# Paired activation parts in the first feed-forward product, and the second norm's sums at a later place, in a two-layer decoder trunk

## The chip, the cores and the metric

The kernel runs on one core of one Trainium2 chip. The metric is device time in microseconds for one execution of the whole program, as the median of several runs. Besides the runs there is one profiled execution, from which all the rows below come.

## The reference, cut to what matters

The input x is 256 tokens by 1024, float32. Two layers each do a normed, gated mix of three token mixers with a residual, and then the feed-forward part, which is where the change lies:

```python
def rms_norm(x, g):
    y = x * lax.rsqrt(jnp.mean(x * x, axis=-1, keepdims=True) + NORM_EPS)
    return y * g

x = x + (g_a * o_a + g_b * o_b + g_c * o_c) @ w_out
h = rms_norm(x, g_ffn)
x = x + jnp.square(jax.nn.relu(h @ w_ff1)) @ w_ff2      # 1024 -> 4096 -> 1024
```

The norm's factor of a row is positive, so it passes through Relu and comes out of the square as its square: the kernel multiplies by g_ffn only, runs both products without the row factor, and multiplies the end result by 1/(mean of squares + eps).

## The kernel before, in words

**Split products.** For float32 accuracy every weight and every activation is held as two parts, hi (the value rounded to the PE's fp32r form) and lo (the rest). A product is three matmuls that add up in one PSUM bank: hi x hi, hi x lo, lo x hi. `gemm_b` (lines 163 to 169) does it with the weights stationary and 256 activation columns moving: line 167 is weight hi with activation hi, 168 weight hi with activation lo, 169 weight lo with activation hi. `gemm_a` (171 to 177) does it with the activations stationary and 512 weight columns moving (lines 175 to 177).

**Weights.** `piece` (143 to 159) fetches 512 KB into a raw buffer (tag raw, five buffers, issued by SP at line 138), ACT writes the hi part (line 157) and DVE the lo part (line 158). Ring 0 has four hi and four lo buffers and holds the first product's weights; ring 1 takes its buffers from the five of tag big.

**PSUM.** `psum` (line 95) hands out whole banks: two of tag mm, two at, two pt, one po, one ch, eight in all. A bank goes to its next user only when everything that reads it is done.

**The feed-forward stage.** After the output projection, `transposed` (203 to 213) transposes x block by block (128 tokens) and writes its hi part (ACT, line 211) and lo part (DVE, line 212), times g_ffn, to h2 and l2, two tiles of 8 x 256 columns. The inner dimension of 4096 is worked in NG = 16 groups of 256, gi = 0 to 15 in the code; the texts below use gi. `ff1(gi)` (893 to 908) runs the first product of a group: two halves u of 128 inner channels, each over 8 chunks k of the model dimension, 2 x 8 x 3 = 48 matmuls into the two halves of one mm bank. In group 0 all u do k 0 to 3 first and then k 4 to 7. Then the result is evacuated: line 903 (ACT) r = Relu, 905 (ACT) rh = Square of r, 906 (DVE) r = max(ps, 0) x r, which reads the bank once more and writes over the r that 905 reads, 907 (DVE) rl = r - rh.

The second product, `acc_pass` (868 to 873), adds a group's part into the four banks po4, two blocks b of tokens by two halves n of the output: 24 matmuls of 512 columns per group. The loop of line 918 issues ff1(gi + 1) ahead of the second product of gi; the second products of the last three groups are kept for the end, so that the first products of groups 14 and 15 run back to back. At the end line 936 (DVE) multiplies by the row factor r2 and adds the residual.

**The second norm's sums.** Lines 912 to 916: for each block `sumsq_row` (232 to 242) does two Squares of 128x512 with an accumulated sum on ACT (line 239), an add and a scale on DVE (240, 241); line 915 takes the reciprocal. They stand between ff1(0) and ff1(1) in the program.

**Order.** Each engine runs its own queue in order. The order in a queue is made ahead of time by a planner that takes, at each point, the oldest instruction whose inputs and buffers it believes to be ready; so an instruction that is younger in the program can stand before an older one that had to wait.

Of the kernel before, what the change touches and what calls it, by code (L numbers as in the profile page):

```python
# [8 lines left out]
F32 = mybir.dt.float32  # L9
R32 = mybir.dt.float32r  # L10
BF16 = mybir.dt.bfloat16
I32 = mybir.dt.int32
AF = mybir.ActivationFunctionType
ALU = mybir.AluOpType
AX = mybir.AxisListType

P = 128
D = 1024
T = 256
NB = T // P  # L20
# [65 lines left out]
def trunk_kernel(ctx: ExitStack, tc: tile.TileContext, A, out, depth=DEPTH):  # L86
    nc = tc.nc
# [3 lines left out]
    ap_ = ctx.enter_context(tc.tile_pool(name="ap", bufs=1))  # L91
# [3 lines left out]
    def psum(tag, name):  # L95
        return pp.tile([P, 512], F32, tag=tag, name=name, bufs={"mm": 2, "at": 2, "pt": 2, "po": 1, "ch": 1}[tag])

    def stat(n, name, dt=F32):
        return sp.tile([P, n], dt, tag="st%d" % n, name=name, bufs=2 if n > 64 else 6)
# [7 lines left out]
    mm = nc.tensor.matmul  # L107
# [35 lines left out]
    def piece(src, k, ring=0, half=0):  # L143

        n = src.shape[-1]
        r = raw(src, n)
        if ring == 0:
            hi = wp.tile([P, 1024], R32, tag="hi", name="hi", bufs=WB)[:, :n]
            if not ringgap:
                ringgap.append(wp.tile([P, 64], F32, tag="gap6", name="gap6", bufs=1))  # L150
            lo = wp.tile([P, 1024], R32, tag="lo", name="lo", bufs=WB)[:, :n]
        else:
            if half == 0:
                ring2[0] = (ap_.tile([P, 2048], R32, tag="big", name="hi2", bufs=BIG),
                            ap_.tile([P, 2048], R32, tag="big", name="lo2", bufs=BIG))
            hi, lo = (t[:, half * 1024:half * 1024 + n] for t in ring2[0])
        act(hi, r, AF.Copy)  # L157
        tt(out=lo, in0=r, in1=hi.bitcast(F32), op=ALU.subtract)  # L158
        return tuple(t.rearrange("p (k n) -> p k n", k=k) for t in (hi, lo))
# [3 lines left out]
    def gemm_b(ps, wh, wl, ah, al, ks, first=True, last=True):  # L163

        n = len(ks)
        for i, (kw, ka) in enumerate(ks):
            mm(ps, lhsT=wh(kw), rhs=ah(ka), start=(first and i == 0), stop=False)  # L167
            mm(ps, lhsT=wh(kw), rhs=al(ka), start=False, stop=False)  # L168
            mm(ps, lhsT=wl(kw), rhs=ah(ka), start=False, stop=(last and i == n - 1))  # L169

    def gemm_a(ps, ah, al, wh, wl, ks, first=True, last=True):

        n = len(ks)
        for i, (kw, ka) in enumerate(ks):
            mm(ps, lhsT=ah(ka), rhs=wh(kw), start=(first and i == 0), stop=False)  # L175
            mm(ps, lhsT=ah(ka), rhs=wl(kw), start=False, stop=False)  # L176
            mm(ps, lhsT=al(ka), rhs=wh(kw), start=False, stop=(last and i == n - 1))  # L177

    def split(hi, lo, src):
        splits[0] = act(hi, src, AF.Copy)  # L180
        splits[1] = tt(out=lo, in0=src, in1=hi.bitcast(F32), op=ALU.subtract)
# [18 lines left out]
                stt(out=y, in0=t, scalar=1.5, in1=y, op0=ALU.add, op1=ALU.mult)  # L200
        return y

    def transposed(src, b, g, hh, hl, name, c0):

        pt = psum("pt", name)
        for c in range(c0, c0 + 4):
            nc.tensor.transpose(pt[:, (c - c0) * P:(c - c0 + 1) * P], src[:, c * P:(c + 1) * P], ident)
        for c in range(c0, c0 + 4):
            pc = pt[:, (c - c0) * P:(c - c0 + 1) * P]
            hc = hh[:, c, b * P:(b + 1) * P]  # L210
            act(hc, pc, AF.Copy, scale=g[:, c:c + 1])
            stt(out=hl[:, c, b * P:(b + 1) * P], in0=pc, scalar=g[:, c:c + 1], in1=hc.bitcast(F32),
                op0=ALU.mult, op1=ALU.subtract)

    scaled = [None]
# [45 lines left out]
    def layer(l):  # L261
# [4 lines left out]
        def K(n, i=None):  # L266
            o, w = COL[n]
            return cols[:, o:o + w] if i is None else cols[:, o + i:o + i + 1]
# [5 lines left out]
        def s2(shape, name, dt=F32):  # L274
            return sp.tile(shape, dt, tag="s2", bufs=S2, name=name)
# [4 lines left out]
        def pa(name, dt=F32):  # L280
            return sp.tile([P, 512], dt, tag="pa", bufs=PA, name=name)
# [2 lines left out]
        hA = lambda t, b: (lambda k: t[:, k, b * P:(b + 1) * P])  # L284
        col = lambda ap: ap.rearrange("p (n o) -> p n o", o=1)


        if l == 0:

            ap_.tile([P, 48], F32, tag="gap0", name="gap0")  # L290
        hh = ap_.tile([P, 8, T], R32, tag="hh", name="hh", bufs=2)
        hl = ap_.tile([P, 8, T], R32, tag="hl", name="hl", bufs=2)
        grow = raw(bass.AP(tensor=A["gmix"].tensor, offset=A["gmix"].offset + l * D, ap=[[0, P], [1, D]]), D)
        vs = stat(2, "n1v")
        for b in range(NB):
# [246 lines left out]
        oh = ol = None  # L542
# [291 lines left out]
        def gated(m, c2):  # L834

            nonlocal mh, ml
            g = gslice(m, c2)
            ps = w_o(("wo_mla", "wconv", "wo_nsa")[m], *((oh, ol, 0), (yh, yl, 0), (oh, ol, 4))[m], c2)
            if m == 1:
                ob = s2([P, 512], "ob")  # L840
                for u in range(2):
                    act(ob[:, u * T:(u + 1) * T], ps[:, u * T:(u + 1) * T], AF.Identity, bias=K("bco", 2 * c2 + u))
                ps = ob
            stt(out=g, in0=g, scalar=1.0, in1=ps, op0=ALU.add, op1=ALU.mult)
            if done[c2]:
                tt(out=g, in0=gslice(done[c2][-1], c2), in1=g, op=ALU.add)
            done[c2].append(m)
            if len(done[c2]) == 3:
                if mh is None:
                    mh = ap_.tile([P, 8, T], R32, tag="hh", name="mh", bufs=2)  # L850
                    ml = ap_.tile([P, 8, T], R32, tag="hl", name="ml", bufs=2)
                c = 2 * c2
                split(mh[:, c:c + 2].rearrange("p c t -> p (c t)"), ml[:, c:c + 2].rearrange("p c t -> p (c t)"), g)

        oh = ap_.tile([P, 8, T], R32, tag="hh", name="oh", bufs=2)
        ol = ap_.tile([P, 8, T], R32, tag="hl", name="ol", bufs=2)
        steps = {"a": a_products, "a0": a_compressed, "a1": a_keys, "a2": a_queries, "qk": nsa_qk, "glu": glu, "lr": low_rank, "lrn": low_rank_norm, "ckv": compress_kv, "csc": compress_scores,
                 "nsa": lambda j: nsa_attention(j, (oh, ol)), "mla": lambda j: mla_attention(j, (oh, ol)),
                 "rk": rotary_keys, "mq": mla_q, "mk": mla_k, "tap": lambda i: taps(TAPS[i], TAPS[i + 1]), "cn": conv_norm,
# [14 lines left out]

        po4 = [[psum("at", "wo0"), psum("at", "wo1")], [psum("po", "wo2"), psum("ch", "wo3")]]
        held = [(k, k) + piece(A["w_out"][l, k], 1, ring=k // 4, half=k % 2) for k in range(8)]
        h2 = ap_.tile([P, 8, T], R32, tag="hh", name="h2", bufs=2)
        l2 = ap_.tile([P, 8, T], R32, tag="hl", name="l2", bufs=2)
        for b in range(NB):
            if b == 0:  # L880
                acc_pass(po4, held, mh, ml, 8, b)
            for n in range(2):
                if b == 1:
                    acc_pass(po4, held, mh, ml, 8, b, (n,))
                xs = x[:, b, n * 512:(n + 1) * 512]
                stt(out=xs, in0=po4[b][n], scalar=0.5, in1=xs, op0=ALU.mult, op1=ALU.add)
                transposed(x[:, b], b, K("gffn"), h2, l2, "n2t", 4 * n)

        po4 = [[psum("at", "f0"), psum("at", "f1")], [psum("po", "f2"), psum("ch", "f3")]]
        NG = 16  # L890
        tail = 3

        def ff1(gi):
            ps = psum("mm", "ff1")
            ws = [piece(A["ff1"][l, 2 * gi + u], 8) for u in range(2)]

            for k0, k1 in ((0, 4), (4, 8)) if gi == 0 else ((0, 8),):
                for u in range(2):
                    wh, wl = ws[u]
                    gemm_b(ps[:, u * T:(u + 1) * T], lambda k: wh[:, k, :], lambda k: wl[:, k, :], hB(h2), hB(l2),  # L900
                           [(k, k) for k in range(k0, k1)], first=(k0 == 0 and (u == 0 or gi > 0)), last=(k1 == 8 and (u == 1 or gi > 0)))
            r = s2([P, 512], "r")
            act(r, ps, AF.Relu)
            rhf, rlf = pa("rh", R32), pa("rl", R32)
            act(rhf, r, AF.Square)  # L905
            stt(out=r, in0=ps, scalar=0.0, in1=r, op0=ALU.max, op1=ALU.mult)
            tt(out=rlf, in0=r, in1=rhf.bitcast(F32), op=ALU.subtract)  # L907
            return tuple(t.rearrange("p (c t) -> p c t", c=2) for t in (rhf, rlf))

        rs = [ff1(0)]  # L910
        r2 = []
        for b in range(NB):
            v = sumsq_row(b, "n2", stat(1, "n2_v"))
            rv = stat(1, "rv")
            nc.vector.reciprocal(rv, v)
            r2.append(rv)
        held = []
        for gi in range(NG):
            if gi + 1 < NG:
                rs.append(ff1(gi + 1))  # L920
            held.append([(2 * gi + u, u) + piece(A["ff2"][l, 2 * gi + u], 1, ring=int(gi < NG - tail + 2), half=u) for u in range(2)])
            if gi < NG - tail:
                for b in range(NB):
                    acc_pass(po4, held[gi], rs[gi][0], rs[gi][1], 2 * NG, b)
# [146 lines left out]
```

## Time and profile before

| what | value |
|---|---|
| time, median of 3 runs | 919.6 us (918.56 to 919.87) |
| the profiled execution's own time | 919.41 us |
| its span, first to last instruction | 917.5 us |
| PE matmul busy | 894.5 us, 97% of the span, 6214 matmuls |
| DVE, ACT busy | 641.9 us (70%), 536.9 us (59%) |
| mean granted TensorE clock | 0.996 of full speed |
| DMA | 151.55 MB, mean 165 GB/s |

Times in the rows count from the span's start. PE is the matmul row of TensorE, PEld its weight loads, DVE the vector engine, ACT the scalar engine, SP the queue that issues the DMAs. L167 is line 167 of the kernel. Matmuls overlap in the pipeline, and their ends are modelled; the start times are measured. An idle time in brackets is followed by what ended it. The feed-forward stages run from 282 to 460 us and from 733 us to the end.

### The profile page before, as it was taken

The numbers are of one execution on the slowest core, as the hardware profiler recorded it, in microseconds if no ns is written. First come the engines' busy times: TensorE is split into PE (matmuls) and PEld (weight loads), VectorE is DVE, ScalarE is ACT, GpSimd is POOL, SyncE is SP. The second block draws the span as 40 slices with busy tenths as digits, with TensorE's granted clock in tenths as the row PEclk, the third lists the DMA queues.
The fourth block names the chain that finished last, engine by engine and source line by source line (L and its number), as shares of the span: only waits on it lengthen the run. The fifth ranks groups of instructions, "written<-read, shape, count | busy, mean of one in ns | idle before, by whom it ended". The sixth has DMA issues, their size and how long they took to land.

```text
span 917.5 us, 16102 instructions
## 1 busy us (share of the span) xinstructions
PE 894.5 (97%) x6214; PEld 794.1 (87%) x6214; DVE 641.9 (70%) x1431; ACT 536.9 (59%) x987; POOL 28.2 (3%) x80
## 2 busy tenths in 40 slices
PE   5999999999999999999999999999999999999998
PEld 4899888689988999999878989877999889999996
DVE  6599988875787665555576999879558785555552
ACT  5456566897467544444354675679865575444430
POOL 4210000000000000000001000000000000000000
PEclk9999999999999999999999999999999999999999
DMA  8654622334656666555355464125436476566621
GB/s 290 217 163 146 221 88 81 115 116 147 186 197 206 217 200 196 191 184 184 103 167 199 162 208 119 61 81 184 160 99 197 151 256 217 185 190 194 190 93 46
DMA packets 43133, 151.55 MB, mean 165 GB/s; under 512 B 4784, under 2 KB 5680, under 8 KB 43056
## 3 DMA queue, kind: packets, MB, share of 16 engines
q1 hardware_dynamic: 43056, 150.52, 50.1%
q8 instruction: 49, 0.80, 0.4%
q14 instruction: 28, 0.23, 0.1%
HBM read 149.45 MB, written 1.05 MB: 164 GB/s over the span
## 4 chain that ended last, share of the span: by engine, by line
PE 86%; DVE 6%; ACT 4%; DMA 3%; issue 1%; SPq 0%; DVEq 0%; ACTq 0%
PE psB L167 7%; PE psB L169 6%; PE psB L168 6%; PE f L177 6%; PE f L175 6%; PE f L176 6%; PE ff L169 6%; PE ff L167 6%; PE ff L168 6%; DVE lo L158 3%; PE wo L167 2%; PE wo L168 2%; PE wo L169 2%; PE nS L589 2%; PE psA L176 2%; ACT hi L157 2%
## 5 line engine op out<-in xcount | busy, mean ns | idle before, releaser
L158 DVE TENSOR_TENSOR lo<-raw,hi 128x1024 fp32r<-128x1024 f32 (+1 forms) x266 | 317.5, 1209 | 168.3 <-ACT hi L157 136.6
L157 ACT ACTIVATE hi<-raw 128x1024 fp32r<-128x1024 f32 (+1 forms) x266 | 273.4, 1048 | 248.1 <-DMA raw<-in_ff_dram 107.3
L167 PE MATMUL psB<-hh,hi 128*128 128x256 f32 x592 | 171.2, 289 | 1.7 <-ACT ug L764 1.4
L169 PE MATMUL psB<-hh,lo 128*128 128x256 f32 x592 | 168.9, 287 | 0.0
L168 PE MATMUL psB<-hl,hi 128*128 128x256 f32 x592 | 168.2, 284 | 0.0
L167 PE MATMUL ff<-h,hi 128*128 128x256 f32 x512 | 143.4, 281 | 0.0
L169 PE MATMUL ff<-h,lo 128*128 128x256 f32 x512 | 143.4, 281 | 0.0
L168 PE MATMUL ff<-l,hi 128*128 128x256 f32 x512 | 143.2, 281 | 0.0
L167 PEld LDWEIGHTS psB<-hh,hi 128*128 128x128 f32 x592 | 112.5, 190 | 8.5 <-issue 4.4
L169 PEld LDWEIGHTS psB<-hh,lo 128*128 128x128 f32 x592 | 112.6, 191 | 3.0 <-issue 2.6
L168 PEld LDWEIGHTS psB<-hl,hi 128*128 128x128 f32 x592 | 112.6, 190 | 0.3
L773 DVE SCALAR_TENSOR_TENSOR ca<-upad,cols,ca 128x256 f32<-128x256 f32 x240 | 103.6, 476 | 0.3
L177 PE MATMUL f<-hi,rl 128*128 128x512 f32 x256 | 100.1, 391 | 1.4 <-DVE n_v L241 1.4
L175 PE MATMUL f<-hi,rh 128*128 128x512 f32 x256 | 100.5, 393 | 0.7 <-ACT rh L905 0.7
L176 PE MATMUL f<-lo,rh 128*128 128x512 f32 x256 | 100.1, 391 | 0.0
L168 PEld LDWEIGHTS ff<-l,hi 128*128 128x128 f32 x512 | 97.8, 191 | 1.0
L167 PEld LDWEIGHTS ff<-h,hi 128*128 128x128 f32 x512 | 96.0, 188 | 1.1
L169 PEld LDWEIGHTS ff<-h,lo 128*128 128x128 f32 x512 | 96.0, 188 | 0.0
L177 PEld LDWEIGHTS f<-hi,rl 128*128 128x128 f32 x256 | 48.1, 188 | 13.0 <-DVE rl L907 2.6
L175 PEld LDWEIGHTS f<-hi,rh 128*128 128x128 f32 x256 | 48.1, 188 | 10.2 <-ACT rh L905 1.1
L176 PEld LDWEIGHTS f<-lo,rh 128*128 128x128 f32 x256 | 48.2, 188 | 9.1
L176 PE MATMUL psA<-lo,hh 128*128 128x512 f32 (+1 forms) x96 | 36.2, 377 | 1.3 <-DVE lo L158 1.3
(279 smaller groups left out, 1421.5 us busy)
## 6 DMA issues: line engine op xcount, KB each, us to landing
raw<-in_ff_dram SPq DMA_DIRECT2D x128, 512.0 KB, 4.1
raw<-in_wB_dram SPq DMA_DIRECT2D x74, 512.0 KB, 3.8
raw<-in_wA_dram SPq DMA_DIRECT2D x16, 512.0 KB, 4.2
raw<-in_w_out_dram SPq DMA_DIRECT2D x16, 512.0 KB, 4.1
raw<-in_wo_nsa_dram SPq DMA_DIRECT2D x8, 512.0 KB, 5.0
raw<-in_wo_mla_dram SPq DMA_DIRECT2D x8, 512.0 KB, 4.4
raw<-in_wconv_dram SPq DMA_DIRECT2D x8, 512.0 KB, 3.8
raw<-in_wA_dram SPq DMA_DIRECT2D x8, 312.0 KB, 5.3
```

Source lines behind the costliest of these rows:

```text
L157: act(hi, r, AF.Copy)
L158: tt(out=lo, in0=r, in1=hi.bitcast(F32), op=ALU.subtract)
L167: mm(ps, lhsT=wh(kw), rhs=ah(ka), start=(first and i == 0), stop=False)
L168: mm(ps, lhsT=wh(kw), rhs=al(ka), start=False, stop=False)
L169: mm(ps, lhsT=wl(kw), rhs=ah(ka), start=False, stop=(last and i == n - 1))
L175: mm(ps, lhsT=ah(ka), rhs=wh(kw), start=(first and i == 0), stop=False)
L176: mm(ps, lhsT=ah(ka), rhs=wl(kw), start=False, stop=False)
L177: mm(ps, lhsT=al(ka), rhs=wh(kw), start=False, stop=(last and i == n - 1))
L589: mm(pS[g].rearrange("p (h z k) -> p h z k", h=nj, z=2)[:, i], lhsT=qTn[gs, 2 * jp + j, b * P:(b + 1) * P], rhs=kTn[gs, :, 0:nk], start=Tr ...
L773: stt(out=ca[:, i], in0=upad[:, i, k:k + T], scalar=K("wdw", 31 * i + k), in1=ca[:, i], op0=ALU.mult, op1=ALU.add)
```

## The change

`ff1` of group 0 stays as it is. In groups 1 to 15 `gemm_p` runs, for each k, one matmul of weight hi with 512 columns, the hi and the lo part of the activations side by side, and one of weight lo with the 256 hi columns, added into the first half of the bank. A half u then fills a whole bank, so a group takes both mm banks. The evacuation adds the two halves of each bank (a copy on ACT and an add on DVE per u), then squares with Relu on DVE and copies the hi part on ACT. For this the hi and lo parts of all activations of that size lie in one tile of [128, 8, 2, 256] instead of two of [128, 8, 256], in as many buffers. The sums of the second norm are issued in the loop, block 0 at gi = 4 and block 1 at gi = 6, behind the weight pieces of that group's second product and ahead of the product; the reciprocal gets a tag of its own.

```diff
+    def gemm_p(ps, wh, wl, a, ks, first=True, last=True):
+
+        n = len(ks)
+        for i, (kw, ka) in enumerate(ks):
+            mm(ps, lhsT=wh(kw), rhs=a[:, ka].rearrange("p s t -> p (s t)"), start=(first and i == 0), stop=False)
+            mm(ps[:, :T], lhsT=wl(kw), rhs=a[:, ka, 0], start=False, stop=(last and i == n - 1))
...
-    def transposed(src, b, g, hh, hl, name, c0):
+    def transposed(src, b, g, h, name, c0):
...
-            hc = hh[:, c, b * P:(b + 1) * P]
+            hc = h[:, c, 0, b * P:(b + 1) * P]
...
+        def pair(name):
+
+            return ap_.tile([P, 8, 2, T], R32, tag="hp", name=name, bufs=2)
...
-        hh = ap_.tile([P, 8, T], R32, tag="hh", name="hh", bufs=2)
-        hl = ap_.tile([P, 8, T], R32, tag="hl", name="hl", bufs=2)
+        hp = pair("hp")
+        hh, hl = hp[:, :, 0], hp[:, :, 1]
...
         def ff1(gi):
-            ps = psum("mm", "ff1")
             ws = [piece(A["ff1"][l, 2 * gi + u], 8) for u in range(2)]
...
+            r = s2([P, 512], "r")
+            rhf, rlf = pa("rh", R32), pa("rl", R32)
+            if gi == 0:
...
+            else:
+                pss = [psum("mm", "ff1") for _ in range(2)]
                 for u in range(2):
                     wh, wl = ws[u]
...
+                    gemm_p(pss[u], lambda k: wh[:, k, :], lambda k: wl[:, k, :], h2, [(k, k) for k in range(8)])
+                for u in range(2):
+                    rt = r[:, u * T:(u + 1) * T]
+                    act(rt, pss[u][:, :T], AF.Copy)
+                    tt(out=rt, in0=pss[u][:, T:], in1=rt, op=ALU.add)
+                stt(out=r, in0=r, scalar=0.0, in1=r, op0=ALU.max, op1=ALU.mult)
+                act(rhf, r, AF.Copy)
             tt(out=rlf, in0=r, in1=rhf.bitcast(F32), op=ALU.subtract)
...
-        for b in range(NB):
-            v = sumsq_row(b, "n2", stat(1, "n2_v"))
-            rv = stat(1, "rv")
-            nc.vector.reciprocal(rv, v)
-            r2.append(rv)
...
+            if gi in (4, 6):
+
+                v = sumsq_row(len(r2), "n2", stat(1, "n2_v"))
+                rv = sp.tile([P, 1], F32, tag="rv", name="rv", bufs=2)
+                nc.vector.reciprocal(rv, v)
+                r2.append(rv)
```

The branch of group 0 holds the old lines, with the old order of k and one bank.

## Rows read from the trace of the kernel before

**Rows 1.** The page, busy time of each engine: us (share of span) xinstructions.
```profile
PE 894.5 (97%) x6214; PEld 794.1 (87%) x6214; DVE 641.9 (70%) x1431; ACT 536.9 (59%) x987; POOL 28.2 (3%) x80
```
**Rows 2.** The page, the chain that ended last, by engine.
```profile
PE 86%; DVE 6%; ACT 4%; DMA 3%; issue 1%; SPq 0%; DVEq 0%; ACTq 0%
```
**Rows 3.** Windows, ten groups: stretch, length, busy us by engine, clock, DMA share, GB/s.
```profile
312.05:423.25 111.20, 111.20 (x721) 101.64 (x720) 62.64 (x64) 52.34 (x60) 0.00 (x0) 1.00 0.61 194
```
**Rows 4.** Timeline, PE, one even group: start, us, engine, line, operation, tiles.
```profile
334.29 0.28 PE L167 MATMUL ff<-h,hi 128*128 128x256 f32 x1
...
339.83 0.28 PE L169 MATMUL ff<-h,lo 128*128 128x256 f32 x1
...
339.94 0.40 PE L175 MATMUL f<-hi,rh 128*128 128x512 f32 x1
...
340.18 0.40 PE L176 MATMUL f<-lo,rh 128*128 128x512 f32 x1
...
341.10 0.39 PE L177 MATMUL f<-hi,rl 128*128 128x512 f32 x1
...
342.46 0.39 PE L177 MATMUL f<-hi,rl 128*128 128x512 f32 x1
```
**Rows 5.** Timeline, PE, group 0 of layer 0.
```profile
284.20 0.28 PE L167 MATMUL ff<-h,hi 128*128 128x256 f32 x1
...
285.56 0.28 PE L167 MATMUL ff<-h,hi 128*128 128x256 f32 x1
```
**Rows 6.** Timeline, ACT, layer 0, around the evacuation of group 0.
```profile
291.63 1.06 ACT L157 ACTIVATE hi<-raw 128x1024 fp32r<-128x1024 f32 x1 [0.29 <-DMA raw<-in_ff_dram]
292.59 0.58 ACT L903 ACTIVATE r<-ff 128x512 f32<-128x512 f32 x1
293.07 0.63 ACT L239 ACTIVATE n_q<-x 128x512 f32<-128x512 f32 x1
...
293.68 0.62 ACT L905 ACTIVATE rh<-r 128x512 fp32r<-128x512 f32 x1
```
**Rows 7.** Timeline, DVE, the last read of group 0's bank.
```profile
294.34 0.69 DVE L906 SCALAR_TENSOR_TENSOR r<-ff,r 128x512 f32<-128x512 f32 x1 [0.39 <-ACT rh L905]
```
**Rows 8.** Timeline, PE, layer 0: last first product of group 1, third second product.
```profile
293.68 0.28 PE L169 MATMUL ff<-h,lo 128*128 128x256 f32 x1
...
295.81 0.50 PE L177 MATMUL f<-hi,rl 128*128 128x512 f32 x1 [0.72 <-DVE n_v L241]
```
**Rows 9.** Timeline, ACT, layer 0, between r and rh of group 1.
```profile
297.47 1.05 ACT L157 ACTIVATE hi<-raw 128x1024 fp32r<-128x1024 f32 x1
298.42 0.62 ACT L905 ACTIVATE rh<-r 128x512 fp32r<-128x512 f32 x1
```
**Rows 10.** Timeline, ACT and PE, the same place in layer 1.
```profile
743.56 0.58 ACT L903 ACTIVATE r<-ff 128x512 f32<-128x512 f32 x1
...
744.77 0.28 PE L169 MATMUL ff<-h,lo 128*128 128x256 f32 x1
...
746.78 0.50 PE L177 MATMUL f<-hi,rl 128*128 128x512 f32 x1 [0.72 <-DVE n_v L241]
```
**Rows 11.** Timeline, ACT and DVE, layer 0, behind the first product of group 14.
```profile
440.11 1.06 ACT L157 ACTIVATE hi<-raw 128x1024 fp32r<-128x1024 f32 x1 [1.77 <-PE ff L168]
441.07 0.58 ACT L903 ACTIVATE r<-ff 128x512 f32<-128x512 f32 x1
...
441.20 1.23 DVE L158 TENSOR_TENSOR lo<-raw,hi 128x1024 fp32r<-128x1024 f32 x1 [1.60 <-ACT hi L157]
```
**Rows 12.** Windows, columns as in rows 3, the stretch at the lower clock.
```profile
119.80:123.20 3.40, 3.40 (x18) 3.40 (x18) 3.30 (x10) 1.71 (x3) 0.12 (x1) 0.50 0.68 171
```
**Rows 13.** Timeline, PE, just before that stretch.
```profile
117.89 1.97 PE L515 MATMUL cS<-kbd,qTn 128*128 128x32 f32 x16
```
**Rows 14.** Windows, a stretch with PE waiting, start of layer 1.
```profile
470.50:473.90 3.40, 1.84 (x8) 0.98 (x7) 1.66 (x3) 1.54 (x2) 0.00 (x0) 1.00 0.85 335
```
**Rows 15.** Timeline, DVE, the last lo part of the activations, layer 0.
```profile
288.11 0.35 DVE L212 SCALAR_TENSOR_TENSOR l<-n2t,cols,h 128x128 fp32r<-128x128 f32 x1 [0.43 <-ACT h L211]
```

More of the change, by code (lines that the diff above doesn't have):

```diff
@@ L209, in transposed @@
             pc = pt[:, (c - c0) * P:(c - c0 + 1) * P]
-            hc = hh[:, c, b * P:(b + 1) * P]
+            hc = h[:, c, 0, b * P:(b + 1) * P]
             act(hc, pc, AF.Copy, scale=g[:, c:c + 1])
-            stt(out=hl[:, c, b * P:(b + 1) * P], in0=pc, scalar=g[:, c:c + 1], in1=hc.bitcast(F32),
+            stt(out=h[:, c, 1, b * P:(b + 1) * P], in0=pc, scalar=g[:, c:c + 1], in1=hc.bitcast(F32),
                 op0=ALU.mult, op1=ALU.subtract)
@@ L849, in gated @@
                 if mh is None:
-                    mh = ap_.tile([P, 8, T], R32, tag="hh", name="mh", bufs=2)
-                    ml = ap_.tile([P, 8, T], R32, tag="hl", name="ml", bufs=2)
+                    mp = pair("mp")
+                    mh, ml = mp[:, :, 0], mp[:, :, 1]
                 c = 2 * c2
-                split(mh[:, c:c + 2].rearrange("p c t -> p (c t)"), ml[:, c:c + 2].rearrange("p c t -> p (c t)"), g)
-        oh = ap_.tile([P, 8, T], R32, tag="hh", name="oh", bufs=2)
-        ol = ap_.tile([P, 8, T], R32, tag="hl", name="ol", bufs=2)
+                split(mh[:, c:c + 2], ml[:, c:c + 2], g.rearrange("p (c t) -> p c t", c=2))
+        op = pair("op")
+        oh, ol = op[:, :, 0], op[:, :, 1]
         steps = {"a": a_products, "a0": a_compressed, "a1": a_keys, "a2": a_queries, "qk": nsa_qk, "glu": glu, "lr": low_rank, "lrn": low_rank_norm, "ckv": compress_kv, "csc": compress_scores,
@@ L876, in layer @@
         held = [(k, k) + piece(A["w_out"][l, k], 1, ring=k // 4, half=k % 2) for k in range(8)]
-        h2 = ap_.tile([P, 8, T], R32, tag="hh", name="h2", bufs=2)
-        l2 = ap_.tile([P, 8, T], R32, tag="hl", name="l2", bufs=2)
+        h2 = pair("h2")
         for b in range(NB):
@@ L886, in layer @@
                 stt(out=xs, in0=po4[b][n], scalar=0.5, in1=xs, op0=ALU.mult, op1=ALU.add)
-                transposed(x[:, b], b, K("gffn"), h2, l2, "n2t", 4 * n)
+                transposed(x[:, b], b, K("gffn"), h2, "n2t", 4 * n)
         po4 = [[psum("at", "f0"), psum("at", "f1")], [psum("po", "f2"), psum("ch", "f3")]]
@@ L893, in ff1 @@
         def ff1(gi):
-            ps = psum("mm", "ff1")
             ws = [piece(A["ff1"][l, 2 * gi + u], 8) for u in range(2)]
-            for k0, k1 in ((0, 4), (4, 8)) if gi == 0 else ((0, 8),):
+            r = s2([P, 512], "r")
+            rhf, rlf = pa("rh", R32), pa("rl", R32)
+            if gi == 0:
+                ps = psum("mm", "ff1")
+                for k0, k1 in ((0, 4), (4, 8)):
+                    for u in range(2):
+                        wh, wl = ws[u]
+                        gemm_b(ps[:, u * T:(u + 1) * T], lambda k: wh[:, k, :], lambda k: wl[:, k, :],
+                               lambda k: h2[:, k, 0], lambda k: h2[:, k, 1], [(k, k) for k in range(k0, k1)],
+                               first=(k0 == 0 and u == 0), last=(k1 == 8 and u == 1))
+                act(r, ps, AF.Relu)
+                act(rhf, r, AF.Square)
+                stt(out=r, in0=ps, scalar=0.0, in1=r, op0=ALU.max, op1=ALU.mult)
+            else:
+                pss = [psum("mm", "ff1") for _ in range(2)]
                 for u in range(2):
                     wh, wl = ws[u]
[L900 to L906, printed above, removed]
+                    gemm_p(pss[u], lambda k: wh[:, k, :], lambda k: wl[:, k, :], h2, [(k, k) for k in range(8)])
+                for u in range(2):
+                    rt = r[:, u * T:(u + 1) * T]
[3 more added lines that the diff above has]
+                act(rhf, r, AF.Copy)
             tt(out=rlf, in0=r, in1=rhf.bitcast(F32), op=ALU.subtract)
```

## Prediction

> **What bounds the kernel now.** I read the page first, then the chain of waits, then the timeline of the two feed-forward stages. On the page TensorE (PE) is busy for 97% of the span [rows 1], and the chain that ended last lies on PE for 86% [rows 2]; in both feed-forward stages it stays on PE from the first second product to the layer's end. So there I count PE's starts: whatever shortens or holds PE's stream moves the end one for one, and work on ACT or DVE counts only where PE waits for it. In the long even stretch of layer 0 that covers ten groups, PE is never idle, DVE is busy 62.6 of 111.2 us and ACT 52.3 [rows 3].
>
> PE's price per matmul is the distance between starts; the durations shown overlap. A group's first product, 48 matmuls of 256 columns, has its first start at 334.29 and its last at 339.83: 5.54/47 = 117.9 ns. In the second product that follows, the first five 512-column matmuls stand 232 ns apart (339.94 to 341.10), the next six 227 ns (341.10 to 342.46) [rows 4]. The 256-column form also runs faster at places: twelve steps from 284.20 to 285.56 are 113 ns each [rows 5].
>
> **The pairing.** Groups 1 to 15 have 2 x 8 sets per layer, 480 in both. A set was three matmuls of 256 columns, 3 x 117.9 = 353.7 ns; it becomes one of 512 and one of 256. The same columns pass, one matmul and one weight load fewer. No row shows the two widths in turns, so I bound it: at best 227 + 113 = 340 ns (13.7 less), at worst 232 + 118 = 350 (3.7 less), and since the very first 512 behind a run of 256 stands 240 ns from the next start [rows 4], nothing gained is the low end; a loss is excluded because nothing is added. I take the middle of best and worst, 345.3, since neither row is nearer to a mixed stream: 8.4 ns x 480 = **4.0 us** gained, ends 0 and 6.6.
>
> Weighed against a page: the rows put the 256-column form 11 ns above 256/2.4 GHz and the steady 512 form 14 ns above 512/2.4. The Trainium skill (TensorE: Matmul & The Clock Gate, "Wait — 56ns, not 53.3ns?") gives a warm matmul a fixed 2.5 ns beyond its columns whatever their number. By that the set would gain one such cost, an estimated 1.2 us in all, and the sum below would be 2.8 higher; the rows show more than that per matmul.
>
> **What the evacuation adds.** Per group ACT's Relu of 128x512 (0.58 us) becomes two copies of 128x256, its Square (0.63) a copy of the same size; DVE gains two adds of 128x256 from PSUM, each between nothing and the 0.69 of its 128x512 form. At most some 0.6 us more on ACT and 1.4 on DVE per group of 11.1 us, where they are busy 5.2 and 6.3: hidden under PE. If that cover were gone, DVE's part alone would cost up to 1.4 x 30 = 42 us.
>
> **The norm's sums, moved.** Each block of 128 rows issues two Squares with their accumulator reads on ACT, an add, a scale and a reciprocal on DVE; no DMA, nothing on SP's or POOL's queue. At gi 4 and 6 they stand in the stretch where ACT is idle for half the time, and their result is read only by L936 at the layer's end: cost nothing (1.5 us a block if ACT were the bound). At the old place one Square stands between r and rh (293.07, 0.62 us) [rows 6], ahead of the chain on which PE waits; what its going is worth depends on what fills its place, next. The new pair layout changes addresses, not sizes: nothing, from the unchanged tile shapes.
>
> **The bank.** The wait I expect is here. There are two "mm" banks. Before, group 0 held one and group 1 the other, so PE could run the whole of group 1 while group 0 was evacuated. Now group 1 wants both: its u=1 half can't start before group 0's bank has been read by L903 and by L906, which comes behind L905. In layer 0 group 0's r starts only at 292.59, behind three weight pieces, the last of which waited for its DMA until 291.63 [rows 6]; L906 takes 0.69 [rows 7].
> PE's supply ends earlier. The first products of groups 0 and 1 end with the start at 293.68 [rows 8], so at 293.80; their last 24 are group 1's u=1 half, 24 x 0.113 = 2.7 us, which is now shut out. PE is through with everything else at 291.1.
> When it resumes: the Square behind r is gone, and ACT's queue will take another ready piece of weights in its place, as it does in the next group, where hi at 297.47 stands between r and rh at 298.42 [rows 9]. Then r at 292.59, 0.48 to the next start, 0.95 for the piece, 0.62 for rh: 294.67. From there PE can run second products on rh while L906 frees the bank. PE stands for 3.6 us. Today it is late by 295.81 - 293.68 less three ordinary steps (0.12 + 0.23 + 0.23), 1.55 us [rows 8]; so 2.0 more. In layer 1 likewise: stream end 744.89 less 24 x 0.118 is 742.05, r at 743.56 gives 745.64, 3.6 us, against 746.78 - 744.77 - 0.58 = 1.43 today [rows 10]: 2.2 more. Together **4.2 us** lost. The ends: 2.4 if nothing is put between r and rh (resuming 0.95 sooner), and a gain of 2.4 if r isn't held behind the pieces (rival 1).
> The Trainium skill (Perfetto Trace Analysis, "Matmuls") speaks against the change in the same place: matmul groups should rotate through PSUM banks so that one's evacuation overlaps the next's matmuls. Without that wait the sum would be 4.2 lower.
>
> In the even stretch the bank is no matter: a half's bank has the second product's 5.47 us of cover, and hi 1.06 + copy 0.58 + lo 1.23 + add 0.69 = 3.6. In groups 14 and 15, which run back to back, the cover is one half, 2.8 us. There a hi goes first on PE's release at 440.11, r starts at 441.07, and lo takes DVE until 442.4 [rows 11]; the add behind it would free the bank 0.2 to 0.4 us late. I take 0.2 us for both layers, ends 0 and 0.8.
>
> **The clock.** The granted clock is at 2.4 GHz nearly throughout. Once, from 119.8 to 123.2, it stands at 0.50, 1.2 GHz [rows 12], right after sixteen 32-column matmuls that took 1.97 us [rows 13]. In another place PE was busy 1.84 of 3.40 us and the clock stayed at 1.00 [rows 14]. No row has PE wholly idle for 3.6 us inside the program; that is emptier than the first place and far from the second, so I give each of the two new waits an even chance to draw such a fall. Price of one: 3.4 us at half speed, **1.7 us**. Likeliest is one of two.
>
> **Sum.** The profiled execution took 919.4 us (span 917.5 and 1.9 around it): 919.4 - 4.0 + 4.2 + 0.2 + 1.7 = 921.5. The median of the runs stands 0.2 above the profiled one: **921.7**, slower by 0.23%. A measurement of this kernel can tell about 0.2% (1.8 us) from no change.
>
> **Rivals.**
> 1. Faster, by ACT's order: r of group 0 is put ahead of the pieces instead of behind. The last l part ends at 288.46 [rows 15]; 14 matmuls later, near 290.1, group 0 is whole, r and rh take 1.1 us, PE resumes at 291.4, 0.3 us after it ran dry, and today's 1.5 us of lateness shrinks by 1.2 in each layer. 919.6 - 4.0 - 2.4 = 913.2. It decides if r starts within a microsecond of group 0's end. For it: r is older than the pieces; against: today the pieces go first, and nothing ahead of that point changes. Chance 0.12.
> 2. Faster, by the pairing: sets at their best (-6.6), nothing between r and rh (+2.4), no fall of the clock: 915.6. Chance 0.11.
> 3. The two cancel: bank wait as forecast without a fall of the clock, 920.0; or the short bank wait, 918.2. Chance 0.32.
> 4. The change doesn't do what it says: the columns are what costs, a set stays at 353.7, and the wait, the tail and one fall are paid in full: 925.7. Chance 0.10.
>
> **How the numbers follow.** The forecast has 0.35. Slower by over 0.2%, it and rival 4: 0.45. Within 0.2%: 0.32. Faster: 0.12 + 0.11 = 0.23. The range goes from 915.5, leaving out most of rival 1, to 925.5, leaving out a pairing worth nothing together with one or two falls; beyond these ends are about 2 in 10. As cases of both signs hold much of it, the forecast's own range is 920.5 to 925.5.
>
> **What would show it.** Right: 512- and 256-column starts of ff in turns, about 345 ns a set; a PE gap of 3 to 4 us ahead of the second product in each layer, released by ACT's rh or DVE's r; a hi between the first r and rh; the even stretch shorter by 0.13 us a group with no gaps; the granted clock at 0.50 behind one gap. Wrong: a set at 340 or 354, a gap under 1.5 us, gaps in every group (evacuation on the path), or time that moved outside the feed-forward stages.

## The result and the profile after

The changed kernel takes **924.27 us** (median, 921.75 to 929.35) against 919.37 (918.30 to 919.98) for the kernel before in the same comparison, ratio 1.0061 with a 95% interval of 1.0040 to 1.0083: slower by about 5 us. Beside the experiments it was run again, on another occasion: 923.13 against 918.03, 1.0059 [1.0039, 1.0080]. The forecast was 921.7 and slower, range 915.5 to 925.5. Sign and range held; the sum behind them held only in part.

The profiled execution of after is the slowest of its runs (929.35 us, span 927.4, mean clock 0.990). The rows below therefore count starts and waits, not the difference of the two spans. Page of after: the engines' busy time, the chain that ended last, and three groups of instructions; in the tiles' names ff is the first product and f the second.

```profile
PE 901.3 (97%) x5734; PEld 777.3 (84%) x5734; DVE 663.3 (72%) x1491; ACT 540.0 (58%) x1017; POOL 27.2 (3%) x80
PE 84%; DVE 7%; DMA 4%; ACT 4%; issue 2%; SPq 0%; DVEq 0%; ACTq 0%
L175 PE MATMUL ff<-h,hi 128*128 128x512 f32 x480 | 172.3, 399 | 0.0
L176 PE MATMUL ff<-h,lo 128*128 128x256 f32 x480 | 135.4, 282 | 0.0
L182 PE MATMUL f<-hi,rh 128*128 128x512 f32 x256 | 101.4, 396 | 4.3 <-ACT rh L917 4.3
```

There are 480 matmuls fewer than in [rows 1], yet PE's busy time hasn't fallen, even less the 5 us that this execution's longer stretches at 1.2 GHz cost (17.0 us of them, shown below, against 6.8). The last line is new: PE now stands 4.3 us ahead of the second product, waiting for ACT's rh. In the kernel before, the same wait stands on two lines of its page, 2.1 us in all:

```profile
L177 PE MATMUL f<-hi,rl 128*128 128x512 f32 x256 | 100.1, 391 | 1.4 <-DVE n_v L241 1.4
L175 PE MATMUL f<-hi,rh 128*128 128x512 f32 x256 | 100.5, 393 | 0.7 <-ACT rh L905 0.7
```

**An even group**, which answers to [rows 4]. Timeline of PE in after: the first product, the second product behind it, and the start of the next group.

```profile
337.89 0.40 PE L175 MATMUL ff<-h,hi 128*128 128x512 f32 x1
...
339.30 0.40 PE L175 MATMUL ff<-h,hi 128*128 128x512 f32 x1
339.53 0.28 PE L176 MATMUL ff<-h,lo 128*128 128x256 f32 x1
339.65 0.40 PE L175 MATMUL ff<-h,hi 128*128 128x512 f32 x1
...
343.54 0.40 PE L182 MATMUL f<-hi,rh 128*128 128x512 f32 x1
...
345.63 0.39 PE L182 MATMUL f<-hi,rh 128*128 128x512 f32 x1
...
349.04 0.40 PE L175 MATMUL ff<-h,hi 128*128 128x512 f32 x1
```

A set takes 339.65 - 339.30 = 0.35 us; over the sixteen sets, 343.54 - 337.89 = 5.65, 353 ns each, is what three 256-column matmuls took. In turns a 512 holds its successor 235 ns (339.30 to 339.53) and a 256 holds its own 118 (339.53 to 339.65). The second product takes 349.04 - 343.54 = 5.50 against 5.47 before: its 232-ns steps last for nine matmuls (343.54 to 345.63) instead of five. So pairing gains 0.01 us per first product and loses 0.035 per second product.

**The bank**, which answers to [rows 6 to 8, 10]. Timeline of PE in after: the two waits, with the last start ahead of each and the blocked half of group 1.

```profile
293.75 0.28 PE L176 MATMUL ff<-h,lo 128*128 128x256 f32 x1
296.02 0.51 PE L182 MATMUL f<-hi,rh 128*128 128x512 f32 x1 [1.99 <-ACT rh L917]
296.36 0.39 PE L183 MATMUL f<-lo,rh 128*128 128x512 f32 x1
...
297.04 0.39 PE L182 MATMUL f<-hi,rh 128*128 128x512 f32 x1
297.26 0.40 PE L175 MATMUL ff<-h,hi 128*128 128x512 f32 x1
...
748.68 0.28 PE L176 MATMUL ff<-h,lo 128*128 128x256 f32 x1
751.32 0.50 PE L182 MATMUL f<-hi,rh 128*128 128x512 f32 x1 [2.36 <-ACT rh L917]
751.65 0.40 PE L183 MATMUL f<-lo,rh 128*128 128x512 f32 x1
```

And ACT's and DVE's timelines at the wait of layer 0:

```profile
291.60 3.08 ACT L157 ACTIVATE hi<-raw 128x1024 fp32r<-128x1024 f32 x3 [0.84 <-DMA raw<-in_ff_dram]
294.59 0.58 ACT L916 ACTIVATE r<-ff 128x512 f32<-128x512 f32 x1
295.07 0.38 ACT L926 ACTIVATE r<-ff 128x256 f32<-128x256 f32 x1
295.33 0.63 ACT L917 ACTIVATE rh<-r 128x512 fp32r<-128x512 f32 x1
...
296.11 0.68 DVE L918 SCALAR_TENSOR_TENSOR r<-ff,r 128x512 f32<-128x512 f32 x1
```

PE's last start is at 293.75, one step later it is out of work, and until 296.02 it waits for rh: 2.15 us, in layer 1 2.52. Five matmuls of the second product then run while L918 reads the bank (until 296.79), and the u=1 half of group 1, which the kernel before would have run in the gap, follows at 297.26. The queue of ACT is as forecast up to r, which stands behind three weight pieces; but between r and rh stands the 0.38-us copy of group 1, not a 1.05-us piece.

**The clock.** Windows of after, columns as in [rows 3]: three stretches at 1.2 GHz, and last the even stretch, which answers to [rows 3] itself.

```profile
752.20:755.60 3.40, 3.40 (x12) 2.82 (x11) 3.22 (x5) 1.49 (x3) 0.00 (x0) 0.50 0.99 311
90.00:96.80 6.80, 6.80 (x31) 6.58 (x32) 3.95 (x24) 2.82 (x9) 0.00 (x0) 0.50 0.92 313
544.00:550.80 6.80, 6.80 (x31) 6.56 (x31) 3.37 (x24) 2.85 (x10) 0.00 (x0) 0.50 0.96 346
312.05:423.25 111.20, 111.20 (x561) 93.93 (x560) 68.84 (x86) 55.95 (x79) 0.00 (x0) 1.00 0.64 190
```

One fall of the clock to 1.2 GHz stands right behind the wait of layer 1. The other two lie outside the feed-forward stages, in code whose arithmetic the change leaves alone; each begins about half a microsecond behind the same run of short matmuls (twelve of one column that take 1.39 us, two of 512 columns, four of 128). They are 13.6 of the 17.0 us at 1.2 GHz in this execution, the slowest. The kernel before has two such falls as well, [rows 12] and another from 570.4 to 573.8; behind the same run of short matmuls, near 90, its clock stayed at 1.00.

### The profile page after: what moved, and what is told of

The parts are those of the page before. It is cut to its first block, busy times and chain, and to the rows that moved or that the text cites. A ratio compares the mean times of both kernels' runs of the same rounds, so it can differ in the third digit from the quotient of the medians.

```text
span 927.4 us, 15225 instructions
## 1 busy us (share of the span) xinstructions
PE 901.3 (97%) x5734; PEld 777.3 (84%) x5734; DVE 663.3 (72%) x1491; ACT 540.0 (58%) x1017; POOL 27.2 (3%) x80
## 3 DMA queue, kind: packets, MB, share of 16 engines
HBM read 149.45 MB, written 1.05 MB: 162 GB/s over the span
## 4 chain that ended last, share of the span: by engine, by line
PE 84%; DVE 7%; DMA 4%; ACT 4%; issue 2%; SPq 0%; DVEq 0%; ACTq 0%
PE ff L175 12%; PE psB L167 7%; PE psB L169 7%; PE psB L168 7%; PE f L182 6%; PE f L184 6%; PE f L183 6%; PE ff L176 6%; DVE lo L158 3%; PE nS L600 2%; PE wo L167 2%; PE wo L168 2%; ACT hi L157 2%; DMA raw<-in_ff_dram 2%; PE wo L169 2%; PE psA L183 2%
## 5 line engine op out<-in xcount | busy, mean ns | idle before, releaser
L167 PE MATMUL psB<-hp,hi 128*128 128x256 f32 x592 | 172.0, 291 | 1.7 <-ACT ug L775 1.4
L175 PE MATMUL ff<-h,hi 128*128 128x512 f32 x480 | 172.3, 399 | 0.0
L169 PE MATMUL psB<-hp,lo 128*128 128x256 f32 x592 | 169.8, 288 | 0.0
L168 PE MATMUL psB<-hp,hi 128*128 128x256 f32 x592 | 168.7, 285 | 0.0
L176 PE MATMUL ff<-h,lo 128*128 128x256 f32 x480 | 135.4, 282 | 0.0
L167 PEld LDWEIGHTS psB<-hp,hi 128*128 128x128 f32 x592 | 113.3, 191 | 8.5 <-issue 4.4
L169 PEld LDWEIGHTS psB<-hp,lo 128*128 128x128 f32 x592 | 113.1, 192 | 3.0 <-issue 2.6
L168 PEld LDWEIGHTS psB<-hp,hi 128*128 128x128 f32 x592 | 113.2, 191 | 0.3
L176 PEld LDWEIGHTS ff<-h,lo 128*128 128x128 f32 x480 | 90.8, 189 | 1.1
L929 ACT ACTIVATE rh<-r 128x512 fp32r<-128x512 f32 x30 | 19.0, 632 | 44.3 <-DVE r L928 44.3
L183 PE MATMUL psA<-lo,hp 128*128 128x512 f32 (+1 forms) x96 | 36.3, 378 | 1.6 <-DVE lo L158 1.6
L182 PE MATMUL psA<-hi,hp 128*128 128x512 f32 (+1 forms) x96 | 36.1, 378 | 1.2 <-ACT hi L157 1.2
```

Source lines behind the costliest of these rows:

```text
L175: mm(ps, lhsT=wh(kw), rhs=a[:, ka].rearrange("p s t -> p (s t)"), start=(first and i == 0), stop=False)
L176: mm(ps[:, :T], lhsT=wl(kw), rhs=a[:, ka, 0], start=False, stop=(last and i == n - 1))
L929: act(rhf, r, AF.Copy)
```

## The experiments

**Theory A:** a set in turns costs what it cost, so pairing gains nothing, and the loss is the wait for group 0's bank in both layers with the clock falls behind it. **Rivals:** the addresses of the paired tiles or the place of the sums carry the loss; the pairing has a price of its own; the first profile's falls were chance.

| kernel | time, us | before beside it | ratio, 95% interval | mean clock of the runs (before's) | PE idle ahead of f, us |
|---|---|---|---|---|---|
| e1 move only | 918.23 | 917.32 | 1.0013 [0.9994, 1.0032] | 0.9973 (0.9972) | 1.9 |
| e2 pairs from group 2 | 921.28 | 917.32 | 1.0042 [1.0024, 1.0061] | 0.9965 (0.9972) | 1.7 |
| e3 grouped | 923.71 | 917.32 | 1.0075 [1.0049, 1.0101] | 0.9930 (0.9972) | 6.1 |
| e4 grouped, from group 2 | 918.20 | 917.32 | 0.9999 [0.9979, 1.0019] | 0.9973 (0.9972) | 2.9 |
| the change again | 923.13 | 918.03 | 1.0059 [1.0039, 1.0080] | 0.9948 (0.9970) | 4.3 |
| e5 layout and move | 919.03 | 918.03 | 1.0010 [0.9995, 1.0026] | 0.9971 (0.9970) | 2.4 |
| e6 two banks, unpaired | 922.19 | 918.03 | 1.0048 [1.0028, 1.0068] | 0.9953 (0.9970) | 4.6 |
| e7 sums in place | 926.03 | 918.03 | 1.0087 [1.0064, 1.0109] | 0.9957 (0.9970) | 5.9 |
| e8 as e2, again | 920.60 | 917.90 | 1.0035 [1.0016, 1.0054] | 0.9972 (0.9971) | 2.1 |
| e9 pairs from group 9 | 919.58 | 917.90 | 1.0014 [0.9998, 1.0030] | 0.9971 (0.9971) | 2.3 |

The last column is the idle time of the page's groups of second products, as shown above for before (2.1) and after (4.3).

**e1: the sums' move alone, on the kernel before.**

```diff
-        for b in range(NB):
-            v = sumsq_row(b, "n2", stat(1, "n2_v"))
...
+            if gi in (4, 6):
+                v = sumsq_row(len(r2), "n2", stat(1, "n2_v"))
```

> Only the sums of the second norm are moved (gi 4 and 6), no pairing, old layout. Theory A (the Square between r and rh held PE at the stage's start): PE's lateness there falls from 1.55 and 1.43 us by up to 0.6 us in each layer, 918.2 us or somewhat under the kernel before, and nothing appears in groups 4 and 6. Rival B (a weight piece of 0.95 us takes the Square's place between r and rh): 0.3 us later in each layer, about 920.0. Rival C (the place doesn't matter): equal to before within 0.5 us.

No difference that can be measured, and PE's idle time is 1.9 us against 2.1. A weight piece of 0.95 us has taken the Square's place between r and rh in both layers, as rival B had it, but without the delay forecast for it.

**e2: the change, with group 1 left in the old form (one bank, 256 columns).** Group 1 then takes one bank and can run while group 0's is read.

```diff
-            if gi == 0:
+            if gi < 2:
...
-                for k0, k1 in ((0, 4), (4, 8)):
+                for k0, k1 in ((0, 4), (4, 8)) if gi == 0 else ((0, 8),):
```

> The change, but group 1 too keeps the old form with one bank, so pairing begins at gi 2 and no half waits for group 0's bank. Theory A (the bank wait is the loss): PE's gaps of 2.3 and 2.6 us ahead of the second product go down to about 1 us or less, no fall of the clock behind them, and the time is that of the kernel before or a little under, 918 to 919.5, since a set in turns of 512 and 256 columns costs the same 353 ns as before. Rival B (the loss lies in clock falls outside the stage or in the new layout): the gaps go but the time stays at 922 to 924.

The bank wait is gone. Timeline of PE in e2, layer 0: where the change's row has 1.99 us in brackets, this one has 0.31.

```profile
293.17 0.28 PE L169 MATMUL ff<-h,lo 128*128 128x256 f32 x1
293.75 0.50 PE L182 MATMUL f<-hi,rh 128*128 128x512 f32 x1 [0.31 <-ACT rh L917]
```

An even group has the same steps as the change (5.644 and 5.502 us), so fourteen paired groups bring no gain. But the runs stay 0.4% above before, more than these steps make, and the interval overlaps that of the change; so by its time alone e2 doesn't show what the wait costs. e8 and e9 come back to this.

**e3: the change, with a half's eight 512s first and its eight 256s behind them.** This takes the two widths out of turns.

```diff
         for i, (kw, ka) in enumerate(ks):
             mm(ps, lhsT=wh(kw), rhs=a[:, ka].rearrange("p s t -> p (s t)"), start=(first and i == 0), stop=False)
+        for i, (kw, ka) in enumerate(ks):
             mm(ps[:, :T], lhsT=wl(kw), rhs=a[:, ka, 0], start=False, stop=(last and i == n - 1))
```

> The change, but within each half u all eight 512-column matmuls run first and then all eight of 256 columns. Theory A (a 512 behind a 256 starts its successor after 235 instead of 227 ns, which eats the gain): only the first one or few 512s of a half are long, a half takes 8 x 227 to 230 + 8 x 116 = 2.74 to 2.77 us instead of 2.82, a group's first product 5.50 instead of 5.64, and the time is 3 to 4 us under that of the change. Rival B (the set's cost isn't in the turns): 5.64 per group again and no difference to the change.

Timelines of e3 (its lines behind the added one are numbered one higher): the second half of an even group on PE, then ACT and PE at the bank wait of layer 0. Last, the window of the clock there.

```profile
341.13 2.03 PE L175 MATMUL ff<-h,hi 128*128 128x512 f32 x8
343.00 1.08 PE L177 MATMUL ff<-h,lo 128*128 128x256 f32 x8
343.92 0.40 PE L183 MATMUL f<-hi,rh 128*128 128x512 f32 x1
```

```profile
292.07 0.58 ACT L917 ACTIVATE r<-ff 128x512 f32<-128x512 f32 x1
292.55 1.05 ACT L157 ACTIVATE hi<-raw 128x1024 fp32r<-128x1024 f32 x1
293.49 0.62 ACT L918 ACTIVATE rh<-r 128x512 fp32r<-128x512 f32 x1
...
294.17 0.79 PE L183 MATMUL f<-hi,rh 128*128 128x512 f32 x1 [3.46 <-ACT rh L918]
```

```profile
293.10:299.90 6.80, 5.74 (x14) 4.47 (x15) 4.21 (x6) 3.29 (x5) 0.00 (x0) 0.50 0.82 282
```

Even grouped, eight 512s stand 1.87 us (234 ns each) and eight 256s 0.92 (115 ns): not the best of either width. By its starts a group's first product takes 5.59 us against 5.65, 1.8 us over thirty groups, and the second product behind it is back at 5.47. And here a piece of weights does slip between r and rh: PE stands for 3.6 us, the wait that the prediction worked out, and a clock fall of 6.8 us stands on its end. So e3 isn't faster than the change although its products are the shorter: the 3 to 4 us forecast for it were missed, since a first product takes 5.59 us instead of 5.50 and the wait grew. The piece between r and rh stands in layer 1 too, where PE stands for 2.8 us.

**e4: e3 with group 1 in the old form.**

> Both edits of the last two runs: pairing from gi 2 on, and all 512s ahead of all 256s in a half. Theory A (turns and bank wait are the two faults): 3.5 to 5 us under the kernel before, 914.5 to 916. Rival B (grouping gains nothing): as the run with pairing from gi 2 alone, about 918 to 919.5.

The long wait is gone, and the whole 0.75% with it: 0.9999, with an interval apart from e3's, which differs by the form of group 1 alone. What grouping saves against the kernel before, 1.7 us over its 28 groups, the runs can't tell from nothing, so no version here beats that kernel, and the 914.5 to 916 of theory A were missed. But e4 against e2 is a test of the turns: the two differ by the order of the widths alone, and e4 is 3.1 us faster (918.20 and 921.28, intervals apart). Timeline of PE in e4, an even group: the starts of a second product, of the first product behind it, and of the next second product.

```profile
339.71 0.40 PE L183 MATMUL f<-hi,rh 128*128 128x512 f32 x1
...
345.17 2.03 PE L175 MATMUL ff<-h,hi 128*128 128x512 f32 x8
...
350.77 0.40 PE L183 MATMUL f<-hi,rh 128*128 128x512 f32 x1
```

The second product takes 5.46 us (e2: 5.50) and the first 5.60 (e2: 5.64). With the last groups, the feed-forward stages of e4's trace are 1.4 us shorter than e2's although PE waits 1.2 us longer in them: 2.6 us of the 3.1.

**The change again, on the chip of the next three.**

> The change itself, unedited, beside the three kernels that follow on one chip. Theory A (a set in turns costs what three 256-column matmuls cost, so pairing gains nothing; the loss is the wait for group 0's bank in each layer and the clock falls behind it): 1.004 to 1.008 times the kernel before; gap ahead of the first second product 2.0 to 2.9 us in each layer. Rival L (the loss is in the addresses of the paired tiles, or in where the sums stand, not in the bank): the same total, but the layout kernel or the kernel with the sums at the old place carries the difference. Rival C (chance clock falls of the first profile): within 0.2% of before.

The loss repeats. Timeline of PE at the two waits of this execution, then the windows of the clock right behind each:

```profile
294.80 0.79 PE L182 MATMUL f<-hi,rh 128*128 128x512 f32 x1 [1.93 <-ACT rh L917]
...
748.77 0.79 PE L182 MATMUL f<-hi,rh 128*128 128x512 f32 x1 [2.34 <-ACT rh L917]
```

```profile
294.80:298.20 3.40, 3.40 (x9) 2.72 (x10) 3.40 (x6) 1.83 (x2) 0.00 (x0) 0.50 0.88 312
748.80:752.20 3.40, 3.40 (x9) 2.72 (x10) 3.40 (x6) 1.80 (x2) 0.00 (x0) 0.50 0.82 258
```

**e5: the change's tiles and the moved sums, all groups in the old form.** As e2, with another bound.

```diff
-            if gi == 0:
+            if gi < NG:
```

> Paired tiles and the moved sums, with all sixteen groups' products and evacuation in the old form. Theory A: within 0.2% of the kernel before (1.000 to 1.002, as the move alone), 0.4 to 0.6% under the change; ff 5.65 us a group, f 5.47, no gap over 1.5 us. Rival L: 1.004 or more, with steps of ff or f longer than before's though nothing in the feed-forward stage has changed but addresses.

1.0010: layout and move together cost 0.9 us by the ratio; the interval goes from nothing to 2.4. The rival that puts the loss there falls.

**e6: the change, unpaired, but with its two banks and its evacuation.**

```diff
-            mm(ps, lhsT=wh(kw), rhs=a[:, ka].rearrange("p s t -> p (s t)"), start=(first and i == 0), stop=False)
+            mm(ps[:, :T], lhsT=wh(kw), rhs=a[:, ka, 0], start=(first and i == 0), stop=False)
+            mm(ps[:, T:], lhsT=wh(kw), rhs=a[:, ka, 1], start=False, stop=False)
```

> The change with each 512-column matmul written as two of 256 columns into the two halves of the same bank: two banks per group and the new evacuation stay, the pairing goes. Theory A: the same time as the change within 0.2% (1.004 to 1.008 over before), ff 5.65 us a group, the same gaps of 2.0 to 2.9 us in both layers. Rival P (pairing has a price of its own, for instance the 0.03 us by which the second products are longer, and more clock falls): faster than the change by 1 to 3 us, f back at 5.47. If pairing did gain something: slower than the change by up to 4 us.

Timeline of PE in e6: the first second product behind each wait (lines numbered one higher).

```profile
291.13 0.50 PE L183 MATMUL f<-hi,rh 128*128 128x512 f32 x1 [1.67 <-ACT rh L918]
...
741.25 0.67 PE L183 MATMUL f<-hi,rh 128*128 128x512 f32 x1 [2.91 <-ACT rh L918]
```

This kernel separates the two parts. With two banks and no pairing it stands 3.2 us above e5 (922.19 - 919.03), which differs from it by the banks and the evacuation only: most of the change's loss, with waits of the same kind, and the two intervals lie apart. Its second products are back at 5.47 us, as rival P had it. Pairing then adds another 0.9 us (923.13 - 922.19) instead of saving any: the steps say some 0.7, and the intervals overlap, so the runs alone can't tell it from nothing.

**e7: the change, with the sums at their old place.**

> The change with the norm's sums at their old place behind group 0. Theory A: the Square stands between group 0's r and rh again (0.62 us), so the gap grows from 2.0 to 2.9 us to 2.6 to 3.5 in each layer: 0.5 to 1.5 us slower than the change, 1.005 to 1.010 over before. Rival S (the moved sums cost something where they stand now): faster than the change by 1 us or more.

Timelines of e7: ACT from r to rh in layer 0, and PE's first second product in both layers (L246 is the norm's Square).

```profile
293.93 0.58 ACT L916 ACTIVATE r<-ff 128x512 f32<-128x512 f32 x1
294.40 0.62 ACT L246 ACTIVATE n_q<-x 128x512 f32<-128x512 f32 x1
...
295.02 0.62 ACT L917 ACTIVATE rh<-r 128x512 fp32r<-128x512 f32 x1
...
295.69 0.50 PE L182 MATMUL f<-hi,rh 128*128 128x512 f32 x1 [2.87 <-ACT rh L917]
...
747.86 0.50 PE L182 MATMUL f<-hi,rh 128*128 128x512 f32 x1 [3.02 <-ACT rh L917]
```

The Square is back between r and rh, PE's idle time grows from 4.3 to 5.9 us, and the kernel's median is 2.9 us above the change's, more than the forecast 0.5 to 1.5; the two intervals overlap. Of the 1.6 us of idle time only 0.7 is the Square's: it holds rh for 0.62 us (294.40 to 295.02) where the copy held it for 0.26, in each layer. The rest is an r that starts later: 10.12 and 10.25 us after the stage's first matmul, against 9.56 and 9.92 in after, and that time differs between the other profiles as well. So the move, worth nothing alone (e1), takes some 0.7 us off the wait that the banks made.

**e8 and e9: e2 again, and e2 with pairing from group 9 on only**, to see whether the 0.42% of e2 was real. The edit is e9's against e2.

```diff
-            if gi < 2:
+            if gi < 9:
```

> The kernel that keeps group 1 in the old form and pairs groups 2 to 15, a second time. Its idle time ahead of the second products was no longer than before's, and its steps account for 1 us, yet its runs stood 0.42% above before. Theory A (the pairing itself costs 0.8 to 1 us through slower starts of the second products, the rest of that 0.42% was chance): 1.000 to 1.002. Rival P (pairing has a further cost of some 3 us that the feed-forward steps don't show): 1.003 to 1.005 again.

> Groups 1 to 8 in the old form, groups 9 to 15 paired: half the pairing, no wait for group 0's bank. Theory A: 1.000 to 1.0015, second products of 5.47 us in the unpaired half and 5.50 in the paired half. Rival P: half of the excess of the kernel that pairs from group 2, about 1.002.

The 0.42% came again: 1.0035. Theory A had put the excess down to chance, and in that it falls; e9, with half of the pairing, lies at 1.0014, and its interval holds both theories. The steps of e8 account for 1.0 us (second products +0.036 x 24, first products -0.009 x 26, the last groups +0.4), layout and move for 0.9 by e5's ratio. Of the 3.2 to 3.9 us, 1.3 to 2 stay open, though e5's interval, which reaches 2.4 us, could hold them: the feed-forward stages of the two profiles don't show them, and outside those stages executions differ by more (the first stage begins anywhere from 280.3 to 285.0 us in the profiles here).

## Why the prediction was right, and where it was wrong

**The pairing was mis-sized, and its sign was wrong.** Forecast: 345.3 ns a set, the middle of best and worst, 4.0 us gained. Measured: 353 ns, the low end. The step that failed is "I take the middle": I had one row on a change of width, the first 512 behind a run of 256 at 240 ns [rows 4], used it only to set the low end, and read the 232- and 227-ns steps of a pure stream as the ends for a mixed one. In turns every 512 is the one behind a 256. That it is the turns that cost is shown by e4 against e2. The set of rival 4 (it stays at 353.7), to which I gave 0.10, is what happened. "A loss is excluded because nothing is added" was wrong as well, since the second products behind the turns were put at nothing: with the slower second products (0.035 us x 26) and the last two groups (below) less the 0.01 x 30, the pairing costs 0.8 us. (The middle of 340 and 350 is 345.0, not 345.3, and the prediction's 294.67 should be 294.64; neither moves the sum by over 0.2 us.)

By the Trainium skill's fixed cost per matmul (TensorE: Matmul & The Clock Gate, "Wait — 56ns, not 53.3ns?") one matmul fewer per set would have gained an estimated 1.2 us. That isn't borne out here: the thirty first products gained 0.3. The Trainium skill's sentence that larger matmuls are more efficient than smaller ones (Perfetto Trace Analysis, "Matmuls") isn't borne out in turns either, where 512 and 256 columns take what three times 256 take; grouped, as in e3 and e4, a first product does take 0.06 us less than before.

**The bank wait was right in place and kind, and too large.** Forecast: PE stands for 3.6 us in each layer, 4.2 more than before. Measured: 2.15 and 2.52. Counted as in the prediction, with the slow step behind the wait (296.02 to 296.36, 0.11 over an ordinary one), that is 2.26 against 1.55 and 2.63 against 1.43: 1.9 in all. What failed is "ACT's queue will take another ready piece of weights in its place": a 0.38-us copy stood there, of which 0.26 came between the starts (295.07 to 295.33), instead of 0.95. The rest is r: it starts 0.72 us after PE has run out (294.59 - 293.87), where taking 24 matmuls off the old trace gave 1.49 (292.59 - 291.1). PE's side was right: it runs out 8.8 us after the stage's first matmul (285.03 in after, 282.35 before), as taken off the old trace. It is r that comes earlier, 9.56 us after that matmul instead of 10.24. In the profiles here this time goes from 9.3 to 10.7 us, with idle times of ACT ahead of the pieces that the landing of their DMAs ended, so the size of the wait differs from execution to execution (2.09 and 2.50 in the change's second). The 3.6-us case exists: e3 has it in layer 0, piece and all.

That the wait is the bank's is shown by e2, e4, e8 and e9 (group 1 on one bank: idle time back at 1.7 to 2.9 us) and by e6 (two banks without pairing: 4.6); that it costs time, by e4 against e3 and e6 against e5. The Trainium skill's rule on rotating through PSUM banks (Perfetto Trace Analysis, "Matmuls"), which the prediction weighed, is borne out by them. Rival 1, in which r goes ahead of the pieces, didn't occur in any run: r stands behind three pieces.

**The clock was right.** Forecast: one fall of two waits, 1.7 us. In the five executions profiled with the two-bank group 1 (the change twice, e3, e6, e7), six of the ten waits have a fall to 1.2 GHz that begins within about a microsecond of the wait's end; in the other seven, none of the fourteen layers' feed-forward stages has one. Counted from PE's running out, the six followed waits of 2.1 to 3.6 us and the other four are waits of 1.8 to 3.0 us, so length alone doesn't sort them. The runs agree: the mean clock of the change's is 0.0022 lower than before's beside them (0.9948, 0.9970), and over the three sets of before's runs a thousandth of clock goes with 0.8 to 1.0 us, so some 2.0 us by that correlation. I also wrote that the clock stood at 0.50 once in the kernel before; its trace has a second such stretch at 570.4.

**The tail and the evacuation.** Forecast 0.2 us for groups 14 and 15, from an add that comes behind a lo. Measured 0.1 in each layer, by that mechanism; DVE's and PE's timelines of after:

```profile
442.25 1.23 DVE L158 TENSOR_TENSOR lo<-raw,hi 128x1024 fp32r<-128x1024 f32 x1 [1.70 <-ACT hi L157]
443.39 0.42 DVE L927 TENSOR_TENSOR r<-ff,r 128x256 f32<-128x256 f32 x1
...
443.87 0.51 PE L175 MATMUL ff<-h,hi 128*128 128x512 f32 x1
444.21 0.28 PE L176 MATMUL ff<-h,lo 128*128 128x256 f32 x1
```

The add ends at 443.81, and the next half starts right behind it, with a first step of 0.34 us instead of 0.235. In the window of the ten even groups DVE has 68.84 us instead of 62.64, 0.6 per group, ACT 55.95 instead of 52.34: inside the bounds, and hidden, since PE is busy all of the 111.20.

**The sum.** Pairing +0.8 (forecast -4.0, and 0.2 for the tail), wait +1.9 (forecast +4.2), clock +2.0 (forecast +1.7): 4.7 against the measured 4.9 and 5.1. Layout and move (0.9 by e5's ratio) and what stayed open in e2 and e8 have no place in this sum, so it is an account from steps, waits and clock, not a closed one. The forecast came out 2.6 us low (924.27 - 921.7): the pairing with its tail was 4.6 too good, the wait 2.3 too bad, and the second error hid half of the first. The range covered that, and that the sign came out right is in part luck; the way to 921.7 didn't hold.

## What to carry to other kernels

Price a mixed stream by its own switches, not by the steps of two pure streams: one row in which the width changes says more than long rows in which it doesn't. Where two widths must be mixed, try them in groups: here that was 3.1 us faster than in turns. Before giving an accumulator a second bank, look for the place where a pool of two is full, here the very first group, and count what PE still has to do until the bank is read. A short wait on a busy PE costs more than its length if the clock falls behind it, so price that fall with a chance of its own.

## What was not expected of the hardware

The same matmul form has two paces in these traces, and the pace goes with what ran before it: 512 columns take 235 ns in turns with 256, 232 for the first nine of a stretch behind those turns, 232 for only five behind plain 256s, and 227 from then on; and eight 256s in a row behind eight 512s take 115 ns each, 118 in turns. The clock falls outside the feed-forward stages wander: two executions of one and the same program have them at 90.0 and 544.0 (6.8 us each), and at 120.7 and 479.1 (3.4 us each). In the kernel before the mean clock goes with most of the spread of its runs: in the set beside the change's second measurement, 915.25 us for a run at a mean clock of 1.000 against 920.92, the mean of two at 0.994.
